# Portions of filler matmuls between attention bursts: a table by job size, or a sum over VectorE's and TensorE's instructions in each interval

## The chip, the cores and the metric

One core of a Trainium2 chip runs the kernel; the time is device microseconds (us) of one execution, and times are given as the median of several. The engines are TensorE (PE in the profile, its weight loads PEld), VectorE (DVE), ScalarE (ACT), GpSimd (POOL) and SyncE (SP), which issues most DMAs. Each runs its own list of instructions and waits on semaphores for the others.

## The reference

Two layers over x of 1024 x 1024, one sequence. Each layer normalises x, modulates it by c, and multiplies it by one wide matrix `w_in` (5912 columns). Two token mixers of eight heads, 64 wide, read the result:

```
stick-breaking (SB):  z = q k^T / 8 over the keys up to the query block's end
                      log_keep = log_sigmoid(-z) before the diagonal, else 0
                      w = exp(log_sigmoid(z) + reversed cumsum(log_keep) - log_keep);  out = w v
sparse (NSA):         out = g0 * (softmax over compressed keys) + g1 * (softmax over the 8 best
                      64-key blocks of each query) + g2 * (softmax over a 256-key window)
```

Each mixer's output is multiplied by a SiLU gate and projected to 1024 columns; the two are merged by sigmoid gates that are further columns of `w_in` (m_a and m_b), projected once more and added to x.

## The kernel before, in words

All matrix products are split into a high and a low half (fp32r), so that a product of 128 x 128 by 128 x 512 is three matmuls: high by high, high by low, low by high (lines 194, 196, 198). `split` makes the halves: ScalarE copies the high half (line 136), VectorE subtracts for the low half (line 137).

A layer runs in order: `early` (part of the projections, all that NSA needs), `nsa`, `sb`, `output`. Fourteen groups of projections that neither needs at once, six for SB's q, k and v and eight for the merge gates, are not run in a block of their own. `queue_projections` makes them generators that yield after each matmul the time planned for it (0.213 us for 512 columns), and `pump(us)` runs them for so many planned us. They are the filler: independent matmuls placed among the attention's. A group is 96 matmuls of 512 columns, or as much in narrower ones.

Attention is a list of jobs. In SB a job is one head and one m of 0 to 3: two blocks of 128 queries, with 256 m + 128 and 256 m + 256 keys. Its part A (`sb_scores`) makes scores in chunks of up to 512 keys; ScalarE takes two sigmoids of each (lines 1298 and 1299, into C and E); after a block's last chunk VectorE runs one product scan over all its keys (line 1302, C) and multiplies (line 1303, E). Its part B transposes E on TensorE in bursts of up to four (line 898, into tr), splits what comes out (wh and wl), and multiplies by the values (lines 917 and 918, the latter with the low half wl); a burst's value product comes three bursts behind its transposes (`lag`). The last step merges (lines 935 and 936).

In NSA a job is a pair of heads and one block i of 0 to 7 of 128 queries (called n0 to n7 below), or the compressed branch of two blocks for four heads (c0 to c3; `nsa_cmp`, from block 4 on with the choice of the best blocks, a chain of short VectorE instructions). Part A of a pair makes scores (lines 885, 886, 888), VectorE adds masks and takes the maximum, ScalarE the exponential (lines 1146 and 1148); part B scales (VectorE at line 1166, ScalarE at 1167), transposes, splits and multiplies by the values as above. Keys, values and queries come from DRAM by DMA, two buffers each; keys and values of the second half of the heads go into the buffers of the first.

`run_jobs` merges part A of job n with part B of job n - 1, item by item: that is an interval, called s0-s1 where B is of m = 0 and A of m = 1. After each item it pumps an equal share of 85% of the interval's budget, and after the last one the other 15% (`tail`). An interval of SB has 5 (s0-s1), 9 (s1-s2), 11 (s2-s3) or 11 items (s3-s0). The budget before is a number that belongs to the job of part B: `nsa_us` by i, `cmp_us`, `sb_us` by m; 3.0 us (`start_us`) in the first interval. A head in SB gets 1.34 + 2.87 + 4.77 + 6.04 = 15.0 planned us.

The order in which `pump` and the items issue their instructions is the written order. A planner (the framework's scheduler, with its own estimates of durations) then settles the order on each engine; where it expects an instruction to wait, it may put a later one in front.

Of the kernel before, what the change touches and what calls it, by code (L numbers as in the profile page):

```python
# [87 lines left out]
class Trunk:  # L88
    def __init__(self, tc, I, O, depth=2, dbg=None):
        self.tc, self.nc, self.I, self.O, self.depth = tc, tc.nc, I, O, depth  # L90
        self.dbg = dbg or {}
        self.n = 0
        self.fill = []
        self.debt = 0.0
        self.clock, self.seq, self.later = 0.0, 0, []
        self.plan, self.at, self.loaded = [], 0, {}

        self.nsa_us = (1.5, 2.4, 3.85, 4.5, 5.6, 6.1, 6.85, 7.3)
        self.sb_us = (1.34, 2.87, 4.77, 6.04)
        self.cmp_us = 1.48  # L100
        self.start_us = 3.0
        self.tail = 0.15

        self.rpd = 7.0
        self.nh0 = 6.0
        self.nhd = 2.5
        self.lag = 3
        self.wbufs = 4
        self.rawb = 3
        self.wb = 6  # L110
        self.trb = 3
        self.scb = 2
        self.adb = 5
# [170 lines left out]
            self.run_gen(self.fill.pop(0)[1])  # L284
        self.debt = 0.0

    def run_jobs(self, jobs):


        for n in range(len(jobs) + 1):  # L290
            B = jobs[n - 1][1] if n else []
            A = jobs[n][0] if n < len(jobs) else []
            us = jobs[n - 1][2] if n else self.start_us
            merged = []
            for x in range(max(len(A), len(B))):
                merged += A[x:x + 1] + B[x:x + 1]
            for f in merged:
                f()
                self.pump(us * (1 - self.tail) / len(merged))
            self.pump(us * self.tail)  # L300
# [686 lines left out]
    def nsa(self, l):  # L987
        tc, nc = self.tc, self.nc
        with tc.tile_pool(name=f"nsa{l}", bufs=2, reuse_waits="tile") as pool:
            kv, qs, cmp = self.kv, self.qs, {}  # L990
            load_kv, load_q = self.nsa_load_kv, self.nsa_load_q

            def cmp_job(n):
                g, m = n // 4, n % 4
                st = {"sel": [None, None], "pg": [None, None]}
                cmp[n] = st
                return ([lambda x=x: self.nsa_cmp(pool, g, m, x, qs[n], st) for x in range(2)],
                        [lambda: None] * 2 + [lambda: self.nsa_cmp_t(pool, st)], self.cmp_us)

            def pair_job(n, hp, x, st):  # L1000

                g, m = n // 4, n % 4
                hs = {}
                A, B = [], []
                if hp == 0 and x == 0:
                    A.append(lambda: load_q(n + 1))
                if m == 3 and hp == 1 and x == 1:
                    A.append(lambda: load_kv(g + 1) if g == 0 else self.sb_first())
                for r in range(2):
                    A += self.nsa_scores(pool, g, m, hp * 2 + r, r, x, lambda: qs[n], lambda: kv[g], cmp[n], hs)  # L1010
                B.append(lambda: self.nsa_scale(pool, g, m, hp, x, hs))
                B += self.nsa_av(pool, g, m, hp, x, lambda: kv[g], cmp[n], hs)

                def fin():
                    if x == 0:
                        st["o"] = self.tl(pool, [64, 2, 256], F32, "o")
                    self.nsa_merge(pool, hs["ps"], st["o"][:, :, x * P:x * P + P])
                    if x == 1:
                        self.nsa_finish(pool, st["o"], g * 4 + hp * 2, m)
                B.append(fin)  # L1020
                return A, B, self.nsa_us[2 * m + x]

            jobs = [cmp_job(0)]
            for n in range(8):
                for hp in range(2):
                    st = {}
                    for x in range(2):
                        if hp == 1 and x == 0 and n + 1 < 8:
                            jobs.append(cmp_job(n + 1))
                        jobs.append(pair_job(n, hp, x, st))  # L1030
            self.run_jobs(jobs)

    def nsa_cmp(self, pool, g, m, x, q, st):

# [212 lines left out]
    def sb(self, l):  # L1247
        tc, nc = self.tc, self.nc
        with tc.tile_pool(name=f"sb{l}", bufs=2, reuse_waits="tile") as pool:
            qkv = self.qkv  # L1250

            def job(head, m, st):
                hs = {}
                A, B = [], []
                for x in range(2):
                    A += self.sb_scores(pool, m, x, lambda: qkv[head], hs)

                def begin():
                    if m == 0:
                        self.sb_load(head + 1)  # L1260
                    hs["ps"] = self.tl(self.pav, [P, 512], F32, "av", bufs=1)
                bursts = self.pipeline(pool, self.av_stages(pool, m, lambda: (hs["e", 0], hs["e", 1]),
                                                            lambda: qkv[head][2]), lambda: hs["ps"], True)
                B.append(lambda: (begin(), bursts[0]()))
                B += bursts[1:]

                def fin():
                    if head % 2 == 0:
                        st[m] = self.tl(pool, [P, 256], F32, f"o{m}", bufs=1)
                    self.merge(pool, hs["ps"], st[m], head % 2)  # L1270
                    if head % 2 == 1:
                        self.finish_pair(pool, st[m], head // 2 * 128, m, 512 + head // 2 * 128)
                B.append(fin)
                return A, B, self.sb_us[m]

            jobs = []
            st = {}
            for head in range(8):
                for m in range(4):
                    jobs.append(job(head, m, st))  # L1280
            self.run_jobs(jobs)

    def sb_scores(self, pool, m, x, qkv, hs):

# [227 lines left out]
```

## Time and profile before

| | |
|---|---|
| median of 3 runs | 2184.01 us (2183.47 to 2190.08) |
| profiled execution | 2188.37 us, its span 2186.6 us |
| TensorE busy | 2096.8 us (96%), mean granted clock 0.990 |
| VectorE busy | 1575.6 us (72%) |
| ScalarE busy | 1130.8 us (52%) |
| NSA, first layer and second | 296.8 to 677.9 and 1361.9 to 1736.1 us |
| SB, first layer and second | 677.9 to 942.1 and 1736.1 to 2000.4 us |

The stretches of the two phases are taken from the timeline: from a phase's first attention matmul to the next phase's first, and for SB to its last value product. A matmul counts as busy from its start to a modelled end, so matmuls that follow each other overlap, and the distance from start to start tells the pace. An idle entry in brackets at the end of a timeline row is how long the engine stood idle before that instruction, and what ended the wait.

### The profile page before, as it was taken

The numbers are of one execution on the slowest core, as the hardware profiler recorded it, in microseconds if no ns is written. First come the engines' busy times: TensorE is split into PE (matmuls) and PEld (weight loads), VectorE is DVE, ScalarE is ACT, GpSimd is POOL, SyncE is SP. The second block draws the span as 40 slices with busy tenths as digits, with TensorE's granted clock in tenths as the row PEclk, the third lists the DMA queues.
The fourth block names the chain that finished last, engine by engine and source line by source line (L and its number), as shares of the span: only waits on it lengthen the run. The fifth ranks groups of instructions, "written<-read, shape, count | busy, mean of one in ns | idle before, by whom it ended". The sixth has DMA issues, their size and how long they took to land.

```text
span 2186.6 us, 36378 instructions
## 1 busy us (share of the span) xinstructions
PE 2096.8 (96%) x12952; PEld 1817.6 (83%) x12952; DVE 1575.6 (72%) x3698; ACT 1130.8 (52%) x2465; POOL 72.4 (3%) x242
## 2 busy tenths in 40 slices
PE   3999999999999999999999999999999999999999
PEld 3899788988988777779799987889898877777899
DVE  5758568878867778786866763887788687778643
ACT  4433137666666656563533422765666656556410
POOL 2200000000000000010001000000000000001000
PEclk8999999999999999999999999999999999999999
DMA  7445933244226454175456465222532444534433
GB/s 292 96 150 169 287 121 103 87 124 126 80 64 149 126 140 125 64 252 180 157 170 167 137 180 150 84 90 86 145 97 83 121 127 113 145 100 167 154 123 104
DMA packets 254102, 297.02 MB, mean 136 GB/s; under 512 B 38888, under 2 KB 201568, under 8 KB 253920
## 3 DMA queue, kind: packets, MB, share of 16 engines
q1 hardware_dynamic: 213152, 250.65, 38.3%
q10 hardware_dynamic: 36224, 29.37, 5.3%
q0 software_dynamic: 4544, 14.68, 2.4%
q8 instruction: 102, 1.67, 0.3%
q14 instruction: 80, 0.66, 0.1%
HBM read 206.28 MB, written 83.89 MB: 133 GB/s over the span
## 4 chain that ended last, share of the span: by engine, by line
PE 72%; DVE 15%; DMA 4%; issue 4%; ACT 3%; POOL 1%; SPq 0%; DVEq 0%; ACTq 0%; POOLq 0%
PE proj L194 16%; PE proj L198 16%; PE proj L196 16%; PE tr L898 6%; DVE C L1302 5%; PE av L918 4%; PE av L917 3%; PE sc L885 3%; PE sc L886 3%; DVE E L1303 3%; DVE wl L137 2%; DVE w L137 1%; ACT wh L136 1%; DMA ada<-in_ada_w 1%; DMA actlo<-AD 1%
## 5 line engine op out<-in xcount | busy, mean ns | idle before, releaser
L194 PE MATMUL proj<-acthi,w 128*128 128x512 f32 x1312 | 537.5, 410 | 3.4 <-DVE sz L833 2.1
L198 PE MATMUL proj<-acthi,w 128*128 128x512 f32 x1312 | 536.9, 409 | 0.8 <-DVE w L137 0.8
L196 PE MATMUL proj<-actlo,w 128*128 128x512 f32 x1312 | 534.5, 407 | 0.5 <-DVE actlo L137 0.5
L136 ACT CAST w<-raw 128x512 fp32r<-128x512 f32 (+1 forms) x296 | 183.5, 623 | 219.4 <-PE proj L198 111.3
L137 DVE TENSOR_TENSOR wl<-tr,wh 128x512 fp32r<-128x512 f32 (+2 forms) x408 | 255.8, 639 | 46.1 <-ACT wh L136 44.4
L194 PEld LDWEIGHTS proj<-acthi,w 128*128 128x128 f32 x1312 | 249.8, 190 | 40.6 <-DVE sz L833 2.5
L196 PEld LDWEIGHTS proj<-actlo,w 128*128 128x128 f32 x1312 | 249.3, 190 | 37.7 <-DVE actlo L137 1.9
L198 PEld LDWEIGHTS proj<-acthi,w 128*128 128x128 f32 x1312 | 249.0, 190 | 37.5 <-DVE w L137 1.3
L136 ACT CAST wh<-tr 128x512 fp32r<-128x512 f32 (+2 forms) x408 | 219.2, 550 | 87.7 <-PE tr L898 84.7
L137 DVE TENSOR_TENSOR w<-raw,w 128x512 fp32r<-128x512 f32 (+1 forms) x296 | 203.3, 690 | 85.0 <-ACT w L136 83.6
L194 PE MATMUL proj<-w,acthi 128*128 128x256 f32 (+1 forms) x768 | 222.0, 289 | 7.1 <-ACT G L813 3.3
L198 PE MATMUL proj<-w,actlo 128*128 128x256 f32 (+1 forms) x768 | 221.3, 288 | 0.0
L196 PE MATMUL proj<-w,acthi 128*128 128x256 f32 (+1 forms) x768 | 220.5, 287 | 0.0
L898 PE MATMUL tr<-ident,E 128*128 128x128 f32 x1152 | 188.7, 275 | 26.1 <-DVE E L1303 25.5
L918 PE MATMUL av<-wl,V 128*128 128x256 f32 (+1 forms) x776 | 202.1, 287 | 5.5 <-DVE wl L137 5.5
L917 PE MATMUL av<-wh,V 128*128 128x256 f32 (+1 forms) x776 | 202.0, 278 | 0.4 <-ACT E L1146 0.2
L898 PEld LDWEIGHTS tr<-ident,E 128*128 128x128 f32 x1152 | 140.3, 140 | 72.0 <-DVE E L1303 40.6
L1302 DVE TENSOR_TENSOR_SCAN C<-C 128x128 f32<-128x128 f32 (+7 forms) x128 | 173.1, 1352 | 34.3 <-ACT C L1298 33.6
L885 PE MATMUL sc<-kk,q 128*128 128x512 f32 (+3 forms) x512 | 174.2, 340 | 2.1 <-DVE mx L1143 0.9
L886 PE MATMUL sc<-kk,q 128*128 128x512 f32 (+3 forms) x512 | 174.5, 341 | 0.0
L918 PEld LDWEIGHTS av<-wl,V 128*128 128x128 f32 x776 | 146.0, 188 | 25.7 <-DVE wl L137 13.0
L917 PEld LDWEIGHTS av<-wh,V 128*128 128x128 f32 x776 | 146.4, 189 | 13.7 <-ACT wh L136 3.2
(250 smaller groups left out, 3911.1 us busy)
## 6 DMA issues: line engine op xcount, KB each, us to landing
raw<-in_w_in SPq DMA_DIRECT2D x168, 256.0 KB, 3.3
ada<-in_ada_w SPq DMA_DIRECT2D x48, 512.0 KB, 5.5
kk<-QK SPq DMA_DIRECT2D x48, 512.0 KB, 7.7
q<-QK ACTq DMA_DIRECT2D x64, 256.0 KB, 4.6
QK<-s SPq DMA_DIRECT2D x32, 512.0 KB, 3.1
MD<-sz SPq DMA_DIRECT2D x64, 256.0 KB, 2.6
QK<-s SPq DMA_DIRECT2D x48, 256.0 KB, 4.2
VD<-s SPq DMA_DIRECT2D x48, 256.0 KB, 2.1
```

The source lines that it names most:

```text
L136: nc.scalar.copy(hi, src)
L137: nc.vector.tensor_tensor(lo, src, hi.bitcast(F32), ALU.subtract)
L194: nc.tensor.matmul(ps, lh, rh, start=(x == 0), stop=False)
L196: nc.tensor.matmul(ps, lh, rl, start=False, stop=False)
L198: nc.tensor.matmul(ps, ll, rh, start=False, stop=(x == n - 1))
L885: nc.tensor.matmul(ps, q, k[:, 0, c0:c1], start=True, stop=False)
L886: nc.tensor.matmul(ps, q, k[:, 1, c0:c1], start=False, stop=not masks)
L898: nc.tensor.transpose(pt[:, x * P:x * P + P], b, self.ident)
L917: nc.tensor.matmul(ps[:, c:d], lhsT, hi[:, a:b], start=(first and x == 0), stop=False, skip_group_check=True)
L918: nc.tensor.matmul(ps[:, c:d], lhsT, lo[:, a:b], start=False, stop=(last and x == n - 1), skip_group_check=True)
L1302: nc.vector.tensor_tensor_scan(rev, rev, rev, 1.0, ALU.mult, ALU.bypass)
L1303: nc.vector.tensor_tensor(e[:, 0:nk], e[:, 0:nk], c[:, 1:nk + 1], ALU.mult)
```

## The change

The tables of budgets go. A new function, `budgets`, adds up for every interval the durations of VectorE's instructions and of TensorE's, from formulas by width, takes the surplus of VectorE times 1.25 (NSA) or 1.16 (SB), not below zero, and spreads what remains of the total equally over the 74 intervals. `run_jobs` takes the list. Nothing else is changed: the jobs, their items, the share of the tail and the filler are the same, and the budgets add up to the filler's 286.3 planned us (before: 290.4).

```diff
--- before.py
+++ after.py
@@ -94,11 +94,6 @@
         self.debt = 0.0
         self.clock, self.seq, self.later = 0.0, 0, []
         self.plan, self.at, self.loaded = [], 0, {}
-
-        self.nsa_us = (1.5, 2.4, 3.85, 4.5, 5.6, 6.1, 6.85, 7.3)
-        self.sb_us = (1.34, 2.87, 4.77, 6.04)
-        self.cmp_us = 1.48
-        self.start_us = 3.0
         self.tail = 0.15
 
         self.rpd = 7.0
@@ -284,13 +279,61 @@
             self.run_gen(self.fill.pop(0)[1])
         self.debt = 0.0
 
-    def run_jobs(self, jobs):
-
-
-        for n in range(len(jobs) + 1):
+    def budgets(self):
+
+
+
+        def pe(n):
+            return max(0.112, 0.000455 * n)
+
+        def ve(n):
+            return 0.15 + 0.00104 * n
+
+        def parts(nk):
+            return [min(512, nk - c) for c in range(0, nk, 512)]
+
+        def splits(blocks):
+            return sum(ve(128 * min(4, blocks - b)) for b in range(0, blocks, 4))
+
+        def nsa(i):
+            nk, nw = 128 * i + 128, min(384, 128 * i + 128)
+            blocks = (nk + nw) // 64
+            A = (4 * (sum(map(pe, parts(nk))) + pe(nw)), 2 * (sum(ve(n) + 0.1 for n in parts(nk)) + ve(nw) + 0.1))
+            B = (pe(128) * blocks + 2 * pe(256) * (blocks // 2 + 1),
+                 0.34 + 2 * (0.22 + 0.00053 * nk) + splits(blocks) + ve(256) + ve(512) / 2)
+            return A, B
+
+        def cmp(m):
+            n = 4 * (8 * m + 8)
+            return (8 * pe(128), 2 * (0.5 + 6 * ve(n) + (2.4 if m >= 2 else 0.0))), (4 * pe(128), ve(512))
+
+        def stick(m):
+            ks = (256 * m + 128, 256 * m + 256)
+            A = (2 * sum(pe(n) for nk in ks for n in parts(nk)) + 0.08, sum(0.13 + 0.0021 * n + ve(n) for n in ks))
+            B = (pe(128) * (4 * m + 3) + 2 * (pe(256) * (2 * m + 1) + pe(128)), splits(4 * m + 3) + 1.5 * ve(256))
+            return A, B
+
+        seqs = []
+        seq = [cmp(0)]
+        for n in range(8):
+            i = n % 4 * 2
+            seq += [nsa(i), nsa(i + 1)] + ([cmp((n + 1) % 4)] if n < 7 else []) + [nsa(i), nsa(i + 1)]
+        seqs.append((seq, 1.25))
+        seqs.append(([stick(m) for _ in range(8) for m in range(4)], 1.16))
+        zero = ((0.0, 0.0), (0.0, 0.0))
+        out = []
+        for seq, per in seqs:
+            seq = [zero] + seq + [zero]
+            out.append([max(0.0, b[1][1] + a[0][1] - b[1][0] - a[0][0]) * per for b, a in zip(seq[:-1], seq[1:])])
+        rest = (14 * 96 * pe(512) - sum(map(sum, out))) / sum(map(len, out))
+        return [[(x + rest) * 0.213 / pe(512) for x in o] for o in out]
+
+    def run_jobs(self, jobs, budget):
+
+
+        for n, us in enumerate(budget):
             B = jobs[n - 1][1] if n else []
             A = jobs[n][0] if n < len(jobs) else []
-            us = jobs[n - 1][2] if n else self.start_us
             merged = []
             for x in range(max(len(A), len(B))):
                 merged += A[x:x + 1] + B[x:x + 1]
@@ -995,7 +1038,7 @@
                 st = {"sel": [None, None], "pg": [None, None]}
                 cmp[n] = st
                 return ([lambda x=x: self.nsa_cmp(pool, g, m, x, qs[n], st) for x in range(2)],
-                        [lambda: None] * 2 + [lambda: self.nsa_cmp_t(pool, st)], self.cmp_us)
+                        [lambda: None] * 2 + [lambda: self.nsa_cmp_t(pool, st)])
 
             def pair_job(n, hp, x, st):
 
@@ -1018,7 +1061,7 @@
                     if x == 1:
                         self.nsa_finish(pool, st["o"], g * 4 + hp * 2, m)
                 B.append(fin)
-                return A, B, self.nsa_us[2 * m + x]
+                return A, B
 
             jobs = [cmp_job(0)]
             for n in range(8):
@@ -1028,7 +1071,7 @@
                         if hp == 1 and x == 0 and n + 1 < 8:
                             jobs.append(cmp_job(n + 1))
                         jobs.append(pair_job(n, hp, x, st))
-            self.run_jobs(jobs)
+            self.run_jobs(jobs, self.budgets()[0])
 
     def nsa_cmp(self, pool, g, m, x, q, st):
 
@@ -1271,14 +1314,14 @@
                     if head % 2 == 1:
                         self.finish_pair(pool, st[m], head // 2 * 128, m, 512 + head // 2 * 128)
                 B.append(fin)
-                return A, B, self.sb_us[m]
+                return A, B
 
             jobs = []
             st = {}
             for head in range(8):
                 for m in range(4):
                     jobs.append(job(head, m, st))
-            self.run_jobs(jobs)
+            self.run_jobs(jobs, self.budgets()[1])
 
     def sb_scores(self, pool, m, x, qkv, hs):
 
```

## Rows read from the trace of the kernel before

**Rows 1.** The page's head and part 1: span, busy time of each engine.

```profile
span 2186.6 us, 36378 instructions
...
PE 2096.8 (96%) x12952; PEld 1817.6 (83%) x12952; DVE 1575.6 (72%) x3698; ACT 1130.8 (52%) x2465; POOL 72.4 (3%) x242
```

**Rows 2.** Windows: stretch, length, busy us of PE, PEld, DVE, ACT, POOL; clock, DMA.

```profile
296.80:677.90 381.10, 378.66 (x2438) 333.46 (x2437) 297.84 (x923) 243.03 (x576) 1.74 (x11) 0.99 0.35 101
677.90:942.10 264.20, 248.38 (x1423) 201.14 (x1422) 209.65 (x280) 162.22 (x358) 11.79 (x70) 1.00 0.44 121
1361.90:1736.10 374.20, 372.18 (x2406) 326.89 (x2404) 296.94 (x920) 242.47 (x576) 1.41 (x10) 1.00 0.36 103
1736.10:2000.40 264.30, 248.47 (x1424) 201.25 (x1422) 209.81 (x280) 162.25 (x358) 8.13 (x64) 1.00 0.44 119
```

**Rows 3.** TensorE's waits, first layer's SB: total us, times, longest.

```profile
PE tr L898 <- DVE E L1303: 12.8, 19, 1.1
PE av L918 <- DVE wl L137: 2.8, 6, 0.9
PE tr L898 <- DVE wl L137: 0.2, 1, 0.2
```

**Rows 4.** TensorE's timeline, second head of SB: start, duration, instruction, count.

```profile
719.21 0.55 PE L898 MATMUL tr<-ident,E 128*128 128x128 f32 x3 [0.59 <-DVE E L1303]
...
725.35 0.27 PE L898 MATMUL tr<-ident,E 128*128 128x128 f32 x1
726.50 0.55 PE L898 MATMUL tr<-ident,E 128*128 128x128 f32 x3 [0.88 <-DVE E L1303]
...
736.21 0.60 PE L898 MATMUL tr<-ident,E 128*128 128x128 f32 x4
```

**Rows 5.** VectorE's timeline, the same head.

```profile
725.49 0.96 DVE L1303 TENSOR_TENSOR E<-E,C 128x768 f32<-128x768 f32 x1
...
734.91 1.23 DVE L1303 TENSOR_TENSOR E<-E,C 128x1024 f32<-128x1024 f32 x1
736.16 0.43 DVE L936 TENSOR_TENSOR o<-av,mt 64x256 f32<-64x256 f32 x1
...
739.61 1.96 DVE L137 TENSOR_TENSOR wl<-tr,wh 128x512 fp32r<-128x512 f32 x3
```

**Rows 6.** TensorE's timeline, the same head: its first scores, filler, last products.

```profile
714.12 0.34 PE L885 MATMUL sc<-kk,q 128*128 128x384 f32 x1
...
733.77 0.45 PE L198 MATMUL proj<-acthi,w 128*128 128x512 f32 x1
...
735.21 0.39 PE L198 MATMUL proj<-acthi,w 128*128 128x512 f32 x1
735.44 0.22 PE L885 MATMUL sc<-kk,q 128*128 128x128 f32 x1
...
743.57 0.28 PE L917 MATMUL av<-wh,V 128*128 128x256 f32 x1
...
746.13 0.34 PE L885 MATMUL sc<-kk,q 128*128 128x384 f32 x1
```

**Rows 7.** VectorE's timeline in NSA: last scaling of jobs n4 and n7.

```profile
564.37 0.54 DVE L1166 TENSOR_SCALAR E<-E,f 128x640 f32<-128x640 f32 x1
...
631.30 0.75 DVE L1166 TENSOR_SCALAR E<-E,f 128x1024 f32<-128x1024 f32 x1
```

**Rows 8.** TensorE's timeline in NSA: transposes of the same two jobs.

```profile
564.97 0.55 PE L898 MATMUL tr<-ident,E 128*128 128x128 f32 x3
...
635.58 0.60 PE L898 MATMUL tr<-ident,E 128*128 128x128 f32 x4
```

**Rows 9.** TensorE's waits in the first layer's NSA: total us, times, longest.

```profile
PE tr L898 <- DVE ib L1094: 0.7, 1, 0.7
...
PE sc L885 <- DMA kk<-QK: 0.2, 1, 0.2
```

**Rows 10.** Groups by line, SB: weight loads; count, busy us, mean ns, idle.

```profile
L194 PEld LDWEIGHTS proj<-acthi,w 128*128 128x128 f32 x186 | 35.5, 191 | 2.6
```

## The prediction

> **What bounds the kernel now.** I read the page first, then the busy time of four stretches, then TensorE's waits in the stretches that the change touches, then the timeline around the longest of them. The page gives TensorE 2096.8 us of a 2186.6 us span [rows 1], so no change of order can be worth more than some 90 us, and the change touches only the two attention phases of each layer. By stretch [rows 2], the sparse phase (NSA) leaves TensorE idle for 381.10 - 378.66 = 2.4 us in the first layer and 2.0 in the second; the stick-breaking phase (SB) leaves 264.20 - 248.38 = 15.8 us in each layer. The reader is to see that almost all the idle time that the change can reach lies in SB. Its cause: 12.8 us in 19 waits of a transpose for E, the product that VectorE writes at line 1303 after the scan of line 1302, and 2.8 us in 6 waits of a value product for the low half of the weights [rows 3]; one more of 0.2 makes 26. The second layer answers with the same three rows.
>
> A wait costs more than its idle row. Transposes that follow each other start 0.11 us apart, and the profile holds one busy for 0.27 [rows 4], so each wait hides 0.16 us more: 15.8 + 26 x 0.16 = 20.0 us a layer, 40 us in all. That is what TensorE loses in SB.
>
> Where they fall: in interval s1-s2 (job m = 2 brings its scores, m = 1 its values) the transposes at 719.21 waited 0.59 us, in s2-s3 those at 726.50 waited 0.88, and in s3-s0 those at 736.21 did not wait, though E was only just done at 734.91 + 1.23 [rows 4, 5]. TensorE meanwhile has plenty of filler in the wrong place: 6.04 planned us behind job m = 3, and 1.34 behind m = 0.
>
> **The change part by part.** It takes away four tables of constants and adds no instruction: the same 286.3 planned us of filler (14 groups x 96 matmuls x 0.213) are handed out in other portions. One planned us is 1.09 real ones, since such matmuls start 0.23 us apart [rows 6]. By the formulas in the diff, a surplus of VectorE over TensorE is summed for each interval, times 1.25 or 1.16, and what remains of the total, (313.1 - 156.4 - 112.8) / 74 = 0.594, goes to every interval alike. For s0-s1: VectorE 4.55, TensorE 1.69, so (2.86 x 1.16 + 0.594) x 0.213 / 0.233 = 3.57. All four, before and after: s0-s1 1.34 and 3.57; s1-s2 2.87 and 4.43; s2-s3 4.77 and 5.51; s3-s0 6.04 and 1.51. A head keeps 15.0 us; SB as a whole goes from 119 to 121, NSA from 167.2 to 165.2. The formulas' prices agree with the trace: 0.13 + 0.0021 x 1024 = 2.28 for a scan.
>
> *SB, transposes of m = 1.* They need E of the last score of interval s0-s1. Behind that score stand three of five equal parts of 85% of the budget and the tail of 15%, 0.66 of it, then the first ninth of the next. Before 0.66 x 1.34 + 0.094 x 2.87 = 1.16, after 0.66 x 3.57 + 0.094 x 4.43 = 2.77: 1.76 real us more cover against a wait of 0.59 + 0.16. It goes; next in line is the score behind it, which is ready.
>
> *SB, transposes of m = 2.* Behind the last score of s1-s2 the cover grows by 0.80 us, behind the second one, from which VectorE works through two scans to the E that ends at 725.49 + 0.96 [rows 5], by 1.44. The wait was 0.88 + 0.16 = 1.04: left over 0 to 0.24, I take 0.1.
>
> *SB, transposes of m = 3.* The cover from the last score stays within 0.05 us (0.54 x 0.74 more, one part of 4.53 x 0.077 less), from the second score it grows 0.3: 0 to 0.1, I take 0.1.
>
> *SB, interval s3-s0, which gives the filler up.* Before its last value product stand nine of eleven parts, so that product can come 9 x 0.077 x 4.53 x 1.09 = 3.4 us sooner after the interval's start. It stands at 743.57, behind the interval's first score at 735.44, and the last low half that it needs ends at 739.61 + 1.96 = 741.57 [rows 5, 6]: 2.0 us to spare, so 1.4 us of new wait. E of m = 3 comes 0.68 us earlier against the interval's start (filler moved ahead of it), and from there VectorE is busy without a pause, so its low halves come 0.7 earlier and 0.7 us of wait are left. Bounds: 0, if the scan and product for 256 columns go behind the low halves; 1.4, if nothing shifts. I take 0.7.
>
> *SB, waits for the low half* lie in the short interval s0-s1, between parts of 0.25 us; the parts become 0.66, and they go. Ends: none left, or all 2.8 + 6 x 0.16 = 3.8 us; I take none.
>
> Sum for SB: 0.1 + 0.1 + 0.7 = 0.9 a head, 7 us a layer in place of 20: 13 us gained a layer, 26 in all. VectorE would then be busy 209.65 of about 251 us [rows 2], 84%, not yet the bound.
>
> *NSA.* The budgets move more here: n6-n7 6.85 to 3.93, n5-n6 6.10 to 3.95, n4-n5 5.60 to 3.81, n3-n4 4.50 to 3.59; n3-c2 4.50 to 10.85, n5-c3 6.10 to 11.35, n0-n1 1.50 to 3.22. There is next to nothing to gain (2.4 us a layer), so the question is what is uncovered. A job's first transposes follow its last window score by way of exponentials, reciprocal and scaling, and the interval before supplies the cover. Ahead of n7's values, n6-n7 gives up 0.53 x 2.92 x 1.09 = 1.7 us of it; E was scaled by 631.30 + 0.75 and first transposed at 635.58, 3.5 us to spare. Ahead of n4's, n3-n4 gives up 0.47 x 0.91 x 1.09 = 0.5, and there is none to spare: the second E ended at 564.91, its transposes followed at 564.97 [rows 7, 8]. But the order already lets scores of the next job go first there, and of the five kinds of wait in the NSA stretch, 2.2 us together (the first and the last are shown), none is for E [rows 9]. For the second half of the heads, keys go into buffers that n7's last scores free; TensorE waited 0.2 us for them [rows 9], and the interval in between gives up 1.7 us of cover, 3.4 in two layers. The loads themselves, on SP's and ACT's queues, stay the same in number and order. Bounds: 4 us gained (all of NSA's idle time), 11 lost (0.5 in each of 12 intervals of n3 and n4 that are as tight, 1 where n7 meets the second half in each layer, the keys). I take a loss of 3, nearest the row on the keys.
>
> Total: 26 - 3 = 23 us. The profiled execution took 2188.4 us (1.8 beside its span) and would take 2165; the runs' median is 2184.0, so 2161.
>
> A rule that would make more of it: the Trainium skill, Perfetto Trace Analysis, section Identifying the Most-Contended Engine, says that TensorE's headroom is read from the share of time that LDWEIGHTS is busy, since matmul busy time misleads. Taken straight, [rows 2] leave 381 - 333 = 48 us in each NSA and 264 - 201 = 63 in each SB, 222 in all. The trace agrees only once the share is measured against packed filler, where a 0.19 us load [rows 10] goes with every 0.23 us: 82% is full. SB then lacks 76 against 82%, 19 us a layer, as the waits say, and NSA at 87% lacks nothing.
>
> **The rivals.** *More gain:* SB's waits go without a new one in s3-s0, and NSA loses its small waits too: 40 + 4, 2140 us. For it: VectorE is idle 54 us in SB. Against it: VectorE runs without a pause from 736.16 to 741.57, the first 5.4 us of s3-s0 (six rows between the two shown, none with an idle entry) [rows 5]. By the rule of the Trainium skill there would be room for it in NSA; the rows show none.
>
> *The wait moves.* In s3-s0 TensorE now has 4.07 us of its own work and 1.65 of filler, about what VectorE needs there. If the order on VectorE puts the scans of the next head ahead of the low halves, the 1.4 us come in full, and the tail of the low halves makes the next interval late by as much: 2.5 us a head, all that was won. 2184 us.
>
> *It doesn't do what it says.* The order on each engine is settled by a planner that may pull filler forward or let it lie. In SB it keeps to the written order (seven filler matmuls in a row, 733.77 to 735.21, end interval s2-s3 [rows 6]; two parts of 0.37 and a tail of 0.72 ask for 6.8), so I give it little: 2184 us.
>
> *Slower: NSA uncovered.* The place is the last window score of a job from n2 on: exponentials on ACT, reciprocal, scaling on VectorE, then the transposes. From these intervals the change takes 44 planned us a layer, 96 real us in two. If more than 27% of them (26 us) had been covering that chain, the kernel gets slower; at 40% the loss is 38 and the time 2184 - 26 + 38 = 2196. For it: n4 is tight. Against it: 3.5 us to spare where most is taken [rows 7, 8], work of the next job that can go first, and the 11 us of my bound above.
>
> **How the numbers follow.** Forecast 0.55, its own range 2148 to 2174 (waits left in s3-s0 of 0 to 1.4, NSA from -4 to +11). More gain 0.10, the wait moves 0.16, not what it says 0.05, slower 0.14. All of the first two and a quarter of the third are faster by over 0.3% (6.5 us, about what runs of this kernel can tell from none): 0.69. The rest of the third and the fourth, and a little of the last, lie within: 0.18. Slower 0.13. The range goes from 2143 to 2188: past the forecast's own low end toward the bigger gain, and up over no change, leaving out the slower case and the tail of the biggest gain.
>
> **What would show it.** In the changed profile: the idle rows of the transposes for E in SB fall from 12.8 us a layer to under 4; those for the low half in s0-s1 vanish, and some appear in s3-s0; the distance between two heads' first scores falls from 32.0 us [rows 6] to about 30.4; NSA stays within 4 us of its length. I am wrong if the SB rows stay (the order didn't follow), if s3-s0 shows over 2 us of waits a head (it moved), or if NSA grows by over 10 us a layer.

## The result, and the profile after

The changed kernel takes 2158.09 us (median of 4 runs, 2157.55 to 2160.12), the kernel before 2183.74 beside it (4 runs, 2180.18 to 2190.08): a ratio of 0.9877, 95% interval 0.9856 to 0.9897, or 25.7 us less; forecast were 23 us less, and 2161. The profiled execution after took 2157.62 us (span 2155.8), near its median. The one before lay 4.6 above its median, so the two spans differ by more than the medians, by 30.8.

Part 1 of the page after, its chain by line (part 4: the work that ended last, followed back), and the transposes' group (part 5) answer to [rows 1]:

```profile
span 2155.8 us, 36389 instructions
PE 2086.7 (97%) x12952; PEld 1817.4 (84%) x12952; DVE 1580.6 (73%) x3698; ACT 1126.4 (52%) x2465; POOL 72.2 (3%) x242
PE proj L189 17%; PE proj L191 17%; PE proj L193 17%; PE tr L941 7%; PE av L961 5%; PE av L960 4%; PE sc L929 4%; PE sc L928 4%; DVE C L1345 1%; DVE w L132 1%; DMA actlo<-AD 1%; DMA gt<-MD 1%; DMA q<-QK 1%; DVE E L1346 1%; DMA raw<-in_w_in 1%
L941 PE MATMUL tr<-ident,E 128*128 128x128 f32 x1152 | 179.5, 275 | 8.8 <-DVE E L1346 6.3
```

The same chain and group in the kernel before:

```profile
PE proj L194 16%; PE proj L198 16%; PE proj L196 16%; PE tr L898 6%; DVE C L1302 5%; PE av L918 4%; PE av L917 3%; PE sc L885 3%; PE sc L886 3%; DVE E L1303 3%; DVE wl L137 2%; DVE w L137 1%; ACT wh L136 1%; DMA ada<-in_ada_w 1%; DMA actlo<-AD 1%
L898 PE MATMUL tr<-ident,E 128*128 128x128 f32 x1152 | 188.7, 275 | 26.1 <-DVE E L1303 25.5
```

Line numbers have moved: 194, 196, 198 are now 189, 191, 193; 898 is 941; 917 and 918 are 960 and 961; 1302 and 1303 are 1345 and 1346; 137 is 132. In the chain VectorE's scan and product had 5% and 3% before; now they have 1% each, and the transposes' idle time for E falls from 25.5 us to 6.3 in both layers together.

Windows of the four stretches after, each from a phase's first score to the next phase's (SB to its last value product), against [rows 2]:

```profile
287.60:659.10 371.50, 371.07 (x2396) 327.82 (x2395) 297.28 (x917) 238.76 (x571) 1.10 (x7) 0.99 0.34 98
659.10:917.60 258.50, 253.46 (x1470) 209.03 (x1468) 213.50 (x288) 165.84 (x364) 12.35 (x74) 1.00 0.50 132
1345.20:1709.60 364.40, 363.91 (x2363) 321.75 (x2362) 296.78 (x914) 238.90 (x571) 1.20 (x8) 1.00 0.34 99
1709.60:1968.60 259.00, 253.63 (x1469) 209.08 (x1468) 213.71 (x288) 165.84 (x365) 8.26 (x66) 1.00 0.49 131
```

TensorE's idle time in SB fell from 15.8 us to 5.0 in the first layer and 5.4 in the second, in NSA from 2.4 and 2.0 to 0.4 and 0.5. The planner now starts SB's first scores inside NSA's last interval, so for lengths I cut at NSA's last value product (675.7 and 1733.9 before, 663.0 and 1713.5 after). Then the 30.8 us are:

```
                                        before           after    difference
start and early, first layer             296.8           287.6          -9.2
NSA, both layers                 378.9 + 372.0   375.4 + 368.3          -7.2
SB, both layers                  266.5 + 266.5   254.6 + 255.2         -23.2
SB's last product to next NSA            419.8           427.6          +7.8
SB's last product to the end             186.2           187.2          +1.0
```

TensorE's waits in SB after, first layer, against [rows 3] (total us, times, longest):

```profile
PE tr L941 <- DVE E L1346: 2.9, 6, 1.6
PE tr L941 <- DVE wl L132: 1.5, 3, 0.6
PE av L961 <- DVE wl L132: 0.5, 1, 0.5
```

26 waits became 10: 4.9 us idle and 10 x 0.16 hidden, 6.5 in all (7 were forecast; 20.0 before). The head that [rows 4 to 6] show looks like this on TensorE after (scores, transposes and last products of jobs m = 2 and 3):

```profile
692.28 0.22 PE L928 MATMUL sc<-kk,q 128*128 128x128 f32 x1
...
715.49 0.60 PE L941 MATMUL tr<-ident,E 128*128 128x128 f32 x4
...
723.12 0.22 PE L928 MATMUL sc<-kk,q 128*128 128x128 f32 x1
723.66 0.60 PE L941 MATMUL tr<-ident,E 128*128 128x128 f32 x4
...
724.63 0.61 PE L941 MATMUL tr<-ident,E 128*128 128x128 f32 x4
725.30 1.03 PE L941 MATMUL tr<-ident,E 128*128 128x128 f32 x7
...
728.59 0.22 PE L960 MATMUL av<-wh,V 128*128 128x128 f32 x1
```

and on VectorE, in s3-s0:

```profile
722.35 1.23 DVE L1346 TENSOR_TENSOR E<-E,C 128x1024 f32<-128x1024 f32 x1
...
727.16 1.15 DVE L132 TENSOR_TENSOR wl<-tr,wh 128x512 fp32r<-128x512 f32 x2
729.36 0.43 DVE L979 TENSOR_TENSOR o<-av,mt 64x256 f32<-64x256 f32 x1 [1.05 <-ACT mt L978]
```

No transpose of this head has an idle entry. In s3-s0 all the transposes now come in the first 3 us and the value products behind them; the last low half ends at 728.31, 5.2 us after the interval's first score (6.1 before), the last value product comes after 5.5 (8.4 before, at 743.80), and VectorE then stands idle for 1.05 us. The row of before for it is

```profile
743.80 0.22 PE L917 MATMUL av<-wh,V 128*128 128x128 f32 x1
```

The distance from this head's first score to the next one's is 30.8 us (32.0 before, 30.4 forecast); from the second head to the eighth it is 31.2 on average (33.0 before).

### The profile page after: what moved, and what is told of

Its sections match the earlier page's. It is cut to its first block, busy times and chain, and to the rows that moved or that the text cites. A ratio compares the mean times of both kernels' runs of the same rounds, so it can differ in the third digit from the quotient of the medians.

```text
span 2155.8 us, 36389 instructions
## 1 busy us (share of the span) xinstructions
PE 2086.7 (97%) x12952; PEld 1817.4 (84%) x12952; DVE 1580.6 (73%) x3698; ACT 1126.4 (52%) x2465; POOL 72.2 (3%) x242
## 4 chain that ended last, share of the span: by engine, by line
PE 79%; DVE 7%; DMA 6%; issue 4%; ACT 2%; POOL 1%; SPq 1%; ACTq 0%; DVEq 0%; POOLq 0%
PE proj L189 17%; PE proj L191 17%; PE proj L193 17%; PE tr L941 7%; PE av L961 5%; PE av L960 4%; PE sc L929 4%; PE sc L928 4%; DVE C L1345 1%; DVE w L132 1%; DMA actlo<-AD 1%; DMA gt<-MD 1%; DMA q<-QK 1%; DVE E L1346 1%; DMA raw<-in_w_in 1%
## 5 line engine op out<-in xcount | busy, mean ns | idle before, releaser
L1345 DVE TENSOR_TENSOR_SCAN C<-C 128x128 f32<-128x128 f32 (+7 forms) x128 | 173.1, 1352 | 23.2 <-ACT C L1341 22.7
L941 PE MATMUL tr<-ident,E 128*128 128x128 f32 x1152 | 179.5, 275 | 8.8 <-DVE E L1346 6.3
```

The costliest lines, as they stand in the source:

```text
L941: nc.tensor.transpose(pt[:, x * P:x * P + P], b, self.ident)
L1345: nc.vector.tensor_tensor_scan(rev, rev, rev, 1.0, ALU.mult, ALU.bypass)
```

## The experiments

By interval I count waits from start to start: how much longer than the pace of packed matmuls (0.23 us for 512 columns) a distance is, where that is 0.15 us or more. The column `last` is the interval behind the last head's scores, in which only values of m = 3 are left; the right-hand column is the sum over the first layer's SB. Mean us per interval, both layers:

```
                      s0-s1  s1-s2  s2-s3  s3-s0  last  one SB (layer 1)
before                 0.34   0.88   1.01   0.22   1.28   20.7
after                  0.07   0.19   0.08   0.33   2.75    7.6
e1 new list, SB alone  0.05   0.04   0.10   0.50   3.08    7.9
e4 scan of half        0.23   0.24   0.12   0      0.62    5.4
e2 NSA alone           0.41   0.90   0.93   0.30   0.60   20.6
e5 s0-s1 alone         0      0      1.23   0.39   1.96   14.4
e6 s3-s0 emptied       0.25   0.15   0      0.10   3.27    6.6
e7 heads reshaped      0.13   0.37   0.06   0.34   0       7.1
e3 3.5 to the last     0.07   0.23   0.20   0.68   0       8.9
e9 7.5 to the last     0.07   0.26   0.21   0.45   0.29    7.8
e10 both together      0.10   0.20   0.11   0.59   0       7.4
```

Of each edit the deciding lines are shown; `...` marks lines left out. Those of e1 that unpack the list into `nsa` and `sb` and return it are not repeated.

**SB's part alone (e1).** The changed kernel with the old budgets in NSA (`old` is 3.0 and then the old tables):

```diff
-        return [[(x + rest) * 0.213 / pe(512) for x in o] for o in out]
+        nsa, sb = [[(x + rest) * 0.213 / pe(512) for x in o] for o in out]
...
+        nsa = old
+        sb = [x * (286.27 - sum(nsa)) / sum(sb) for x in sb]
+        return nsa, sb
```

> The new budgets in SB alone, the old table in NSA (SB's list scaled by 0.983 so that the total stays 286.3). Theory (the gain is SB's waits for E and for the low half; the output behind it gives a part back): 2157 to 2163 us, TensorE's idle rows in SB under 7 us a layer. Rival (half of the gain or more comes from NSA's redistribution): 2168 us or more. Rival (NSA was uncovered and the full change is slower than SB's part alone): under 2154.

2163.08 us, ratio 0.9909 (0.9896 to 0.9923): 19.4 less than the 2182.45 of before, just past the weak end of the theory (2157 to 2163). SB has the length of the changed kernel, 254.7 and 255.0 us; behind it 3.9 and 1.4 us are lost again.

**NSA's part alone (e2).** New budgets in NSA, old ones in SB:

```diff
+        sb = [3.0] + [1.34, 2.87, 4.77, 6.04] * 8
```

> The new budgets in NSA alone, the old table in SB (the last SB interval then finds 3.9 planned us of filler instead of 1.9). Theory: NSA was covered all along, so 2178 to 2186 us, SB's rows of 12.8 and 2.8 us as before. Rival (NSA uncovered): 2190 or more. Rival (NSA is half of the gain): 2172 or less.

2173.44 us, ratio 0.996 (0.9948 to 0.9973): 9.0 less. My theory, that NSA was covered all along (2178 to 2186), is wrong, and neither rival holds. NSA is 3.6 and 3.1 us shorter than before, and of its five kinds of wait one is left, here in the first layer:

```profile
PE tr L1123 <- DVE cpg L1116: 0.3, 1, 0.3
```

The 9.0 us are not all NSA's: with less filler spent in NSA, SB's last interval finds 3.9 planned us in place of 1.9, and its wait falls from 1.28 to 0.60 us. The ratios of the two parts multiply to 0.9909 x 0.996 = 0.987, against 0.9877 for both; since e2's last interval is not that of the changed kernel, the two are not its exact halves.

**A smaller scan in the kernel before (e4).** The scan covers the later half of the keys only, so the rest of SB's weights come out otherwise:

```diff
-                rev = c[:, nk - 1::-1]
+                rev = c[:, nk - 1:nk // 2 - 1:-1]
```

> The kernel before with the scan over only the later half of a block's keys, so the output is not the reference's: VectorE's 86.5 us of scans a layer become about 45. Theory (SB's waits are VectorE's chain of scan and product, which the filler failed to cover): the 19 waits for E go almost all, 30 to 40 us off, 2144 to 2154. Rival (the waits come from the order in which the planner put the instructions, whatever VectorE takes): less than 12 us off, 2172 or more.

2150.8 us, ratio 0.9854 (0.9838 to 0.9869): 31.7 less, as the theory has it. The window of its first SB:

```profile
678.20:926.30 248.10, 245.02 (x1424) 201.82 (x1422) 176.09 (x281) 160.15 (x357) 11.79 (x70) 1.00 0.47 130
```

Against [rows 2] VectorE has 33.6 us less to do, and SB is 16.1 shorter: the length goes with the waits (20.7 to 5.4), not with VectorE's load. The chain through the scan was what TensorE waited for. The change gets 13 of those 15 us back with VectorE as busy as before.

**Interval s0-s1 alone (e5).** Old tables, but s0-s1 gets what the change gives it, taken from s3-s0:

```diff
+        sb = [3.0] + [3.57, 2.87, 4.77, 3.49] * 8
```

> The old tables with one number moved: s0-s1 gets 3.57 planned us as in the change, taken from s3-s0 (6.04 to 3.49, so that the last interval keeps the 1.9 that it had). Theory (each wait has its own cover): the waits of m = 1's transposes in s1-s2 and for the low half in s0-s1 go, 1.2 us a head of the 2.45 that start-to-start distances show, 16 heads: 16 to 20 us off, 2162 to 2167. Rival (VectorE is late as a whole, and the wait moves to m = 2's and m = 3's transposes): 5 to 10 us off, 2172 to 2178, with the rows for E in s2-s3 grown.

2169.16 us, ratio 0.9934 (0.992 to 0.9949), between theory and rival. The waits of s0-s1 and s1-s2 are gone, more than one interval's: E of m = 1 comes from s0-s1, and what is late there is late in the next. But a third of the gain moves on. In s2-s3 the transposes wait more than before; in the second head:

```profile
724.69 0.55 PE L949 MATMUL tr<-ident,E 128*128 128x128 f32 x3 [0.87 <-DVE E L1354]
```

**No filler in s3-s0 (e6).** The changed kernel, s3-s0 at zero, the 1.5 us spread over the other three:

```diff
+        add = sb[4] / 3 * 7 / 8
+        sb = [x if n in (0, 32) else 0.0 if n % 4 == 0 else x + add for n, x in enumerate(sb)]
```

> The changed kernel with no filler at all in s3-s0 (its 1.51 planned us spread over the three other intervals of a head, 0.44 each). Theory (the forecast's own term: what s3-s0 gives up there is waited out for the low halves): cover before the last value product falls by 1.1 us, E comes 0.4 earlier, so 0.6 to 0.8 us more of wait a head in the 14 intervals, 8 to 12 us slower than the changed kernel, 2166 to 2170. Rival (once the other three are covered it does not matter where the rest lies): 2155 to 2161.

2156.48 us (2155.16 to 2157.05), ratio 0.9876 (0.986 to 0.9891), that of the changed kernel. My theory, 0.6 to 0.8 us a head more, falls; the rival holds. The wait in s3-s0 goes down, from 0.33 to 0.10. TensorE in that interval of the second head:

```profile
725.55 0.22 PE L931 MATMUL sc<-kk,q 128*128 128x128 f32 x1
...
726.54 1.04 PE L944 MATMUL tr<-ident,E 128*128 128x128 f32 x8
...
728.86 0.33 PE L932 MATMUL sc<-kk,q 128*128 128x384 f32 x1
...
729.78 0.48 PE L189 MATMUL proj<-acthi,w 128*128 128x512 f32 x1
730.10 0.39 PE L191 MATMUL proj<-actlo,w 128*128 128x512 f32 x1
...
730.91 0.22 PE L963 MATMUL av<-wh,V 128*128 128x128 f32 x1
```

Between its first score and its last value products stand two filler matmuls only; transposes, value products and the next job's 384-column scores fill it in turns, and none has an idle entry. What comes back in s0-s1 (0.07 to 0.25) is less: a head waits 0.50 us in all, 0.67 after the change.

**Heads reshaped (e7).** The changed kernel with s0-s1 to s3-s0 at 2.65, 4.37, 5.65, 1.97 and 4.04 planned us in the last interval:

```diff
+        t = (2.7, 4.45, 5.75, 2.0)
+        tail = 4.04
+        k = (sum(sb) - sb[0] - tail) / (8 * sum(t) - t[3])
+        sb = sb[:1] + [t[n % 4] * k for n in range(31)] + [tail]
```

> The changed kernel with 4.0 planned us in SB's last interval and the heads at 2.65, 4.37, 5.65 and 1.97 (for 3.57, 4.43, 5.51 and 1.51), after the spare time that the changed kernel's trace shows (1.0 to 1.2 us between E and the transposes of m = 1, under 0.3 at m = 2 and m = 3). Theory: against the kernel with 3.5 moved to the last interval (2151.4) the waits of s3-s0, 0.68 us a head, are halved: 4 to 6 us faster, 2145 to 2148. Rival (what is left is VectorE's pace, not its cover): 2150 to 2153.

2150.28 us (2149.35 to 2153.05), ratio 0.985 (0.9834 to 0.9866), so the rival. The four waits of a head sum to 0.90 us (0.67 after): nothing is won in the heads; the 2.75 in the last interval are.

**NSA pushed further (e8).** The changed kernel with NSA's budgets between two pair jobs halved from n2 on, the rest raised alike:

```diff
...
+        nsa = [nsa[n] / 2 if n in heavy else nsa[n] + give for n in range(41)]
```

> The changed kernel with the budgets of NSA's intervals between two pairs from n2 on halved again (3.1 to 4.0 becomes 1.6 to 2.0) and the rest given to the other intervals alike, 1.3 each. Theory (the chain of exponentials has 1 to 2 us to spare behind n6 and n7, next to none behind n3 to n5): 1 us less cover, waits of 0.3 to 0.6 us in some 24 of the 46 halved intervals, 6 to 14 us slower than the changed kernel, 2164 to 2172. Rival (the planner's order fills these waits with the next job's scores): 2156 to 2161. Rival (NSA was on the edge all along): 2180 or more.

2161.91 us, ratio 0.9904 (0.989 to 0.9919), 3.8 above the changed kernel and hardly apart from it by the intervals, between the theory (2164 to 2172) and the rival (2156 to 2161). 17 intervals a layer are halved, 34 in all and not the 46 of the expectation. Windows of its two NSA stretches:

```profile
291.50:662.70 371.20, 370.45 (x2398) 327.31 (x2397) 296.19 (x916) 239.88 (x570) 1.12 (x7) 1.00 0.34 98
1344.50:1710.60 366.10, 365.19 (x2365) 322.48 (x2364) 295.43 (x913) 239.50 (x570) 1.21 (x8) 1.00 0.34 99
```

0.75 and 0.9 us idle. There was cover left for another cut of this size. That the next job's scores fill in, as the rival says, is likely but not shown by itself. The slower rival is tested at about twice the change's cut in these intervals and does not come.

**Filler moved to SB's last interval (e3).** 3.5 planned us, 0.11 from each of the other 32 intervals:

```diff
+        sb = [x - 3.5 / 32 for x in sb[:-1]] + [sb[-1] + 3.5]
```

> The changed kernel with 3.5 planned us taken evenly from SB's other 32 intervals (0.11 each) and given to its last one, which has 0.54. Theory (the first waits of the output, 1.7 + 0.5 + 0.7 + 1.1 us behind the first layer's SB, show because no filler is left there): 4 to 8 us faster than the changed kernel, 2150 to 2154. Rival (those waits hang on loads that start when SB's tiles come free, so they move along with the filler): 2156 to 2160.

2151.39 us (2150.84 to 2154.03), ratio 0.9859 (0.9846 to 0.9873): as the theory has it. TensorE's waits behind the first SB in the changed kernel (917.6 to 1011.4):

```profile
PE proj L189 <- DVE gt L1505: 2.9, 3, 1.7
PE proj L189 <- ACT yh L131: 2.5, 1, 2.5
PE proj L189 <- ACT gt L1503: 1.1, 1, 1.1
PE proj L189 <- DVE res L1479: 0.3, 1, 0.3
```

and in this one (918.6 to 1011):

```profile
PE proj L189 <- DVE gt L1507: 0.9, 2, 0.5
PE proj L189 <- ACT gt L1505: 0.8, 1, 0.8
PE proj L189 <- DVE res L1481: 0.6, 2, 0.5
PE proj L193 <- DVE yl L132: 0.2, 1, 0.2
```

6.8 us became 2.5, and the last interval's own waits went (2.75 to 0). The heads lost 0.5 us each for it.

**Twice as much there (e9).** `7.5` in place of `3.5`.

> The changed kernel with 7.5 planned us moved into SB's last interval, 0.23 from each of the other 32 of SB, per layer (twice what the run with 3.5 moved). Theory, the place behind SB's last head was short of filler and 3.5 already closed it: nothing more is won there, and 0.23 x 1.09 = 0.25 us less cover in each other interval costs at most 0.1 to 0.2 in the two of a head that wait: 2150 to 2155, no better than the 2151.4 with 3.5. Rival, more was missing there than 3.5 gave (the last interval's own waits of 2.75 us a layer remain): another 2 to 5 us, 2146 to 2149.

2151.99 us (2151.24 to 2154.14), ratio 0.9861 (0.9843 to 0.9878): no more is won, as the theory had it. But the waits behind SB are back at 5.7 us; the largest are

```profile
PE proj L189 <- DVE gt L1507: 2.9, 3, 1.3
PE proj L189 <- ACT yh L131: 1.6, 1, 1.6
```

So these do not simply shrink with the filler in front of them (what they go with is told below).

**Both (e10).** The last interval at 5.5 and the heads at 3.2, 4.6, 5.9 and 0.8 before scaling, in the lines of e7.

> The changed kernel with SB's heads at 3.2, 4.6, 5.9, 0.8 (scaled to the same total) and 5.5 planned us in the last interval, per layer: the emptied s3-s0 and the fuller last interval put together. Theory, the two gains add up (s3-s0 needs almost no filler; the last interval does): 0.15 us less wait in each head's first three intervals, 7 to 8 us for the last interval, so 2145 to 2150 and the fastest so far. Rival, they share one gain (what is won behind the last head is won once, and the heads have nothing left): 2150 to 2154.

2148.98 us (2145.09 to 2152.44), ratio 0.9839 (0.982 to 0.9858): faster than the changed kernel (its slowest run is below that one's fastest), in the theory's range, and the lowest median of all. But its runs overlap those of e7 and e3 and reach into the rival's range, so it is not told apart from them. SB is 250.0 us in both layers (some filler falls behind its end, so this is not all won), and the stretch from there to the next NSA 427.0, as long as in the changed kernel. The two gains do not clearly add.

## Why the prediction was right, and where not

*SB, the main term, was right in mechanism and size.* 13 us a layer were forecast from waits; start to start they fell by 13.1 in the first layer and 12.8 in the second. By length the two SB stretches gave 23.2, with four more filler matmuls in each (0.9 us) than before. Its steps one by one, per head: m = 1 in s1-s2 was to go to nothing and has 0.19; m = 2 in s2-s3 was to keep 0.1 and has 0.08; the low halves in s0-s1 were to go and 0.07 is left of 0.34. e5 shows the first step by itself, e4 that E behind the scan was the cause. The step that I left out is the last interval, behind the last head: its filler falls from 1.9 planned us to 0.5, and it waits 2.75 us in place of 1.28. That the sum came out (7 forecast, 7.6 and 7.9 measured) is partly luck: what s3-s0 waits less than forecast, the last interval waits more.

*SB, s3-s0: the place was right, the term too large.* 0.7 us a head was taken, of 0 to 1.4; it is 0.33. I shifted E by 0.68 us and kept the order of the rest. Over the seven such intervals of a layer E ends 0.5 us earlier on average and the low halves 1.3 (0.9 in the head shown): with the filler gone, the transposes moved together to the interval's front. With no filler at all (e6) the wait is smaller still, 0.10. But it does not simply follow the filler: it is 0.68 in e3, with 1.4 planned us there, and 0.59 in e10, with 0.8. What e6 shows is that emptying the interval costs nothing; that filler is in the way there is not shown. The rival in which the wait moves here (2184) is refuted.

*NSA: the sign was wrong.* A loss of 3 was taken and 7.2 are won by length (6.7 in e2), beyond my bound of 4. It is not filler moved out of the stretch: between the same cuts it holds 968 filler matmuls in both kernels and both layers. The rival of the bigger gain had this right. Two steps failed. The bound counted idle rows alone, although I had added 0.16 us to each wait in SB; start to start the waits of 0.15 and more came to 7.8 and 5.2 us before, and 4.3 and 2.4 after. (Some 2 us of each first-layer figure are no wait but matmuls at half clock: the granted clock was 0.52 from 303.7 to 308.2 us before, and 0.51 from 294.5 to 299.0 after.) And the loss was taken from the row on the keys, as if what a long interval gives up were missed there. The changed kernel's waits over 287.6 to 663.0 are one row, against [rows 9]:

```profile
PE tr L1121 <- DVE cpg L1114: 0.3, 1, 0.3
```

The wait on the keys is gone, not longer. What went lay mostly in intervals that got more: n5-c3 from 0.56 us to 0, n0-n1 from 0.22 to 0.06, and part of n3-c2. But n7-n0, which had about 0.4, has none either, and its budget falls from 7.3 to 2.6; why its waits went is open. Little new came in n4 to n7, which gave the filler (two waits of some 0.3 us a layer); e8 takes another 31 planned us a layer from n2 on for about 4 us.

*The output behind SB was not in the prediction.* It costs 8.8 us, 7.8 of them in the first layer. Of these, 4.5 are waits: 6.8 us as shown under e3, against 2.3 in the kernel before (942.1 to 1030):

```profile
PE proj L194 <- DVE gt L1462: 1.2, 1, 1.2
PE proj L194 <- DVE res L1436: 1.1, 2, 0.9
```

About 2 more are a stretch of half clock behind the longest of them (below). Behind the filler left over from SB, TensorE's instructions stand in the same order in all the kernels; VectorE's and ScalarE's do not. Up to some 50 us behind SB they stand otherwise than in the kernel before in the changed kernel, e1, e6, e8 and e9, and these five have the wait for yh, of 1.6 to 2.5 us, and the half clock behind it. In e2, e3, e5, e7 and e10 the order is that of before from some 8 us on, yh costs at most 0.5, and the clock stays at 1.00. The last interval's budget alone does not decide it (e9 has the most of all). Nor is the order all: the stretch takes 427.0 us in e10 and 422.5 in e3, and what makes that difference is open.

*The start was not either.* Of the 30.8 us between the profiles, 9.2 lie before any attention, where the order on every engine is the same in both. Over all twelve profiles this part takes 287.6 to 296.9 us, and 296.9 is e4's, which in it is the kernel before, instruction for instruction. So I do not put it down to the change, and the medians, 5.1 us less apart, agree in part. It is not settled, though: the two profiles of the start as it was in the kernel before (its own and e4's) are the longest of the twelve, and both profiled runs lay above their kernel's median, by 4.6 and 6.2 us. e5, with the changed kernel's start, takes 293.9. What makes it vary was not tried.

So the medians' 25.7 stand against 23: SB 23.2 by length, NSA 7.2, less 8.8 behind SB, and some 4 at the start that are not explained. Two errors, NSA's sign (10) and the output left out (9), nearly cancel: that the total came so close to the forecast is luck in part.

*The share of weight loads.* The Trainium skill, Perfetto Trace Analysis, section Identifying the Most-Contended Engine, reads TensorE's headroom from LDWEIGHTS (and from MFU, the arithmetic done as a share of the peak, which is not used here). After, SB stands at 209.03 of 258.5, 81% against the 82% of packed filler: some 3 us lacking, where the waits say 6.5. NSA was at 87% and is at 88%: it did have the few microseconds that I denied it.

## What to carry to other kernels

Measure by interval what the slower engine needs behind the last independent instruction, and give the filler there. An interval in which the fast engine's own work overlaps the chain may go without: here one was emptied at no cost (e6). Count waits from start to start in every phase, also where the idle rows seem too small to matter. And follow such a redistribution past its last interval: what stands behind the phase was ordered anew on two engines, and in these profiles it took back 8.8 of 30.4 us.

## What the hardware showed beyond that

One wait of 2 us can cost more than itself. TensorE in the changed kernel's output, and the windows around it:

```profile
974.51 0.43 PE L189 MATMUL proj<-w,yh 128*128 128x256 f32 x1 [2.45 <-ACT yh L131]
...
976.93 0.41 PE L193 MATMUL proj<-w,yl 128*128 128x256 f32 x1
977.14 0.41 PE L189 MATMUL proj<-w,yh 128*128 128x256 f32 x1
...
978.41 0.28 PE L191 MATMUL proj<-w,yh 128*128 128x256 f32 x1
978.53 0.28 PE L193 MATMUL proj<-w,yl 128*128 128x256 f32 x1
```

```profile
917.60:974.00 56.40, 50.35 (x233) 39.91 (x231) 38.58 (x63) 28.24 (x51) 2.19 (x4) 1.00 0.65 216
974.00:979.00 5.00, 4.41 (x22) 3.94 (x23) 3.62 (x11) 1.65 (x3) 0.54 (x1) 0.66 0.44 143
979.00:1011.00 32.00, 31.75 (x270) 31.55 (x269) 20.30 (x50) 7.81 (x14) 0.00 (x0) 1.00 0.58 185
```

Matmuls of 256 columns start 0.21 us apart and, from 978.2 on, 0.12: the granted clock is at half (1.2 of 2.4 GHz) for some 3.5 us behind a wait of 2.45, in a stretch in which TensorE was busy 50.35 of 56.40 us before it. That costs some 1.7 us beside the wait. In e3, which has no such wait there, the clock stays at 1.00, and in e7, where yh is waited for 0.49 us, too. The length of the wait alone doesn't tell it: one of 1.73 us at 924.29 in the changed kernel lies in the first of these windows, at 1.00, but behind the wait for yh the clock falls in e1, e6, e8 and e9 as well (1.9, 2.3, 1.8 and 1.6 us). The window of e9:

```profile
970.00:980.00 10.00, 8.20 (x53) 7.62 (x52) 6.39 (x17) 3.02 (x6) 0.54 (x1) 0.83 0.59 206
```

The start of the kernel before shows the same with another wait, at 0.43 us for 512 columns in place of 0.23:

```profile
254.58 0.80 PE L194 MATMUL proj<-acthi,w 128*128 128x512 f32 x1 [2.09 <-DVE sz L833]
```

Windows around it, in the kernel before

```profile
240.00:270.00 30.00, 27.09 (x104) 21.15 (x104) 11.16 (x13) 4.88 (x8) 0.00 (x0) 0.89 0.99 267
```

and about the same place in the changed kernel, which has no such wait there and runs more matmuls (118) in less time:

```profile
236.00:263.00 27.00, 27.00 (x118) 21.74 (x117) 11.45 (x14) 4.78 (x8) 0.00 (x0) 1.00 1.02 297
```

The DMA engines are at their full share in both (0.99 and 1.02). A clock of 0.89 over 30 us is 6.6 us at half, or 3.3 lost, of the 9.2 there. e4 and e5 have that stretch at half clock too, near 254 us; these three are the longest starts of the twelve.
